# Norm arithmetic between the stages: from GpSimd to VectorE and ScalarE

## The chip, the cores and the metric

The kernel runs on one core of a Trainium2 chip. The core has five engines, each with its own instruction queue that it works off in order: TensorE (PE, matmuls and transposes; PEld is its weight load), VectorE (DVE), ScalarE (ACT), GpSimd (POOL) and SyncE (SP, which issues most of the DMAs). The metric is the device time of one execution in microseconds (us); of several runs the median is taken.

## What is computed

The reference is a transformer of three layers over 512 latent rows (and in its first layer 256 context rows) of 1024 columns. Each layer mixes the rows (windowed attention, a gated scan, then attention beside a state-space model) and sends them through an MLP or a mixture of experts. What matters here lies between these stages:

```python
def rms_norm(x, gain):
    xf = x.astype(jnp.float32)
    y = xf * lax.rsqrt(jnp.mean(xf * xf, axis=-1, keepdims=True) + NORM_EPS)
    return (y * gain.astype(jnp.float32)).astype(x.dtype)

def modulate(x, gain, shift, scale):
    return rms_norm(x, gain) * (1 + scale) + shift

def channel_mlp(h, w_in, w_out):
    return jnp.square(jax.nn.relu(h @ w_in)) @ w_out
```

After a stage with the result y, the rows become x = x + gate * rms_norm(y, gain), and the next stage reads h = modulate(x, ...). So there are two norms in a row at each change of stage: one over y (below: the postnorm) and one over the new x (the prenorm). All of it is in float32.

## The kernel before

**Precision.** A float32 matmul is made of three matmuls in a faster format. Each operand is split into a high half (a rounding cast, made by ScalarE) and a low half (the operand minus the high half, a subtraction of two tiles); then high x high, high x low and low x high are summed. For weights, `unit` does that for a block of 128 x 2048: the DMA brings `raw`, ScalarE casts `whi` (L233), VectorE subtracts `wlo` (L234). For the normed rows the high half is written at L321 and the low half at L322, into the tile pair `hl` (latent rows) or `hc` (context rows).

**Tiles.** Rows are worked on in tiles of 128: tiles 0 to 3 are latent, 4 and 5 are context. A stage's last matmuls go tile by tile. `finish` of a tile is issued one tile behind the matmuls that make it, so the norms of tile i stand beside the matmuls of tile i + 1, and those of the last tiles stand beside the first matmuls of the next stage.

**One tile's norms.** Postnorm: ScalarE squares y and sums the row (L331); `rsqrt` scales the sum on VectorE (L276) and takes the power -1/2 on GpSimd (L278, here called the root). Where y is in PSUM in two halves (after the out-projections) VectorE does L348 and L349 for each. Where y is one SBUF tile `acc` (after an MLP), one of two forms runs: with `pool`, GpSimd multiplies y by the gate (L342) and VectorE adds y times the root to x (L343); without it, VectorE does L339, which needs the root, and L340. Prenorm: ScalarE squares x (L291), VectorE L276, GpSimd the root, VectorE scales the row into `xn` (L300), TensorE transposes its eight 128 x 128 blocks (L308), and the columns of the result are scaled (and shifted) into the float32 scratch tile `h`: the first `dv` of the eight by VectorE (L312 or L314), the others by ScalarE (L317 or L319). Then the cast L321 and the subtraction L322, both of which read `h`.

**Buffers and order.** The scratch tiles junk, xn and h have one buffer each, so a tile's columns wait until L322 of the tile before has read h. The order of the instructions in each engine's queue is set when the kernel is built, by a scheduler that runs a timeline of all engines; a changed instruction can so move its neighbours. The first matmuls of layer 1 are those of `natproj` (L464 to L471): L468 is high x high, L469 high x low of the weights, L471 the low half of the rows. Accumulations of the MLP's result are L836.

Of the kernel before, what the change touches and what calls it, by code (L numbers as in the profile page):

```python
# [159 lines left out]
class Kern:  # L160
# [130 lines left out]
        self.nc.scalar.activation(junk[:, :n], x, AF.Square, accum_out=ss)  # L291
        return ss

    def prenorm(self, x, scale, shift, h, col, wide=True, dv=0, pool=False):

        nc = self.nc
        hi, lo = h
# [21 lines left out]
                nc.scalar.activation(f[:, k, :], b, AF.Identity, scale=scale[:, k:k + 1], bias=shift[:, k:k + 1])  # L319
        d = slice(col, col + P)  # L320
        self.norms.append((nc.scalar.copy(hi[:, :, d], f).ins, scaled))  # L321
        (nc.gpsimd if pool else nc.vector).tensor_sub(lo[:, :, d], f, hi[:, :, d].bitcast(F32))  # L322

    def postnorm(self, x, y, gate, pool=True):

        nc = self.nc
        ss2 = self.tiny(2)
        w = D // len(y)
        for n, b in enumerate(y):
            junk = self.s.tile([P, D], BF, tag="junk", name=self.nm("junk"))  # L330
            nc.scalar.activation(junk[:, :w], b, AF.Square, accum_out=ss2[:, n:n + 1])  # L331
        ss = ss2[:, 0:1]
        if len(y) == 2:
            ss = self.tiny(1)
            nc.vector.tensor_add(ss, ss2[:, 0:1], ss2[:, 1:2])  # L335
        r = self.rsqrt(ss, 1, D)
        if len(y) == 1:
            if not pool:
                nc.vector.scalar_tensor_tensor(y[0], y[0], r, gate, op0=ALU.mult, op1=ALU.mult)  # L339
                nc.vector.tensor_add(x, x, y[0])  # L340
                return
            nc.gpsimd.tensor_mul(y[0], y[0], gate)  # L342
            nc.vector.scalar_tensor_tensor(x, y[0], r, x, op0=ALU.mult, op1=ALU.add)  # L343
            return
        for n, b in enumerate(y):
            d = slice(n * w, n * w + w)
            t = self.s.tile([P, D], F32, tag="pn", name=self.nm("pn"))[:, d]
            nc.vector.scalar_tensor_tensor(t, b, r, gate[:, d], op0=ALU.mult, op1=ALU.mult)  # L348
            nc.vector.tensor_add(x[:, d], x[:, d], t)  # L349
# [508 lines left out]
def layer0(K):  # L858
# [5 lines left out]
    h = [None, None]  # L864
    hp, h_close = K.opened(K.left("h1l"))
    h[0] = K.pair(hp, "hl", [P, KC, L])
    pre = lambda i, sc, sh, wide=True, dv=0, pool=False: K.prenorm(X[i], sc[:, i // 4], sh[:, i // 4], h[i // 4], i % 4 * P, wide, dv, pool)
    with K.scratch(), K.right("gate") as gp:
        gates = []

        def finish(i, bs):
            if not gates:
                gates.extend(K.mod_gate(0, "mix", b, gp) for b in range(2))
            K.postnorm(X[i], bs, gates[i // 4])
            if i < 4:
                pre(i, sc, sh, dv=0, pool=i < 3)

        def loads():
            for i, x in enumerate(X):
                K.nc.sync.dma_start(x, A["x"][i] if i < 4 else A["ctx"][i - 4])  # L880
        out_full(K, A["w_o0"], [(i, ol, i) for i in range(4)] + [(4 + i, oc, i) for i in range(2)], finish,
                 pre=w_o, loaded=loads)
    K.opool.close()
    h[1] = K.pair(h_close.enter_context(K.left("h1c")), "hc", [P, KC, NCTX])
    with K.scratch(), K.right("gate") as gp:
# [11 lines left out]

        def finish2(i, y):
            K.postnorm(X[i], y, gates2[i // 4])
            pre(i, *K.aff[1, "mix"], dv=2, pool=i < 4)  # L900
        mw, mw_close = K.opened(K.left("mw"))
        mlp(K, 0, list(h), [4, 2], finish2, swap, "left", filler=K.mod_dots(gp, mw), steps=4)
    K.ctx_close.close()
# [274 lines left out]
def layer1(K, X, h, ssm):  # L1178
# [5 lines left out]
    with K.scratch(), K.right("gate") as gp:  # L1184
        gates = []

        def finish(i, bs):
            if not gates:
                gates.append(K.mod_gate(1, "mix", 0, gp))
            K.postnorm(X[i], bs, gates[0])  # L1190
            K.prenorm(X[i], sc[:, 0], sh[:, 0], h3, i * P, dv=3 if i > 1 else 0, pool=i < 1)
        out_full(K, K.A["w_o1"], [(i, oT, i) for i in range(4)], finish)
    K.opool.close()
    h = []
    with K.scratch(), K.right("gate") as gp:
# [8 lines left out]
            h.extend(K.pair(hp, "hl", [P, KC, L]))  # L1204

        def finish2(i, y):
            K.postnorm(X[i], y, gates2[0], i not in (0, 1, 3))
            K.prenorm(X[i], K.sm("mix_gain"), None, h, i * P, dv=2, pool=i < 3)
        tp, t_close = K.opened(K.left("ssmt"))
        mlp(K, 1, [h3], [4], finish2, swap, "left", True, ssm.constants(tp))  # L1210
    return h
# [939 lines left out]
```

## Time and profile before

| | us |
|---|---|
| median of 3 runs | 2224.25 |
| lowest, highest run | 2215.38, 2228.82 |
| the profiled execution: its time, its span | 2222.53, 2220.7 |
| TensorE busy | 2111.7 (95%) |
| VectorE busy | 1388.7 (63%) |
| ScalarE busy | 968.0 (44%) |
| GpSimd busy | 333.4 (15%) |
| mean granted TensorE clock | 0.980 |

The span runs from the first to the last instruction. In the rows, "0.39 PE L468 ..." is one instruction (or, with x2, several in a row) with its duration; "[1.61 <-DVE xn L300]" says that the engine was idle for 1.61 us before it, and what ended that. The granted clock is 1.00 at full speed (2.4 GHz) and 0.5 at the lower of its two levels (1.2 GHz); between these it is a mean over the window.

### The profile page before, as it was taken

The page shows a single profiled execution, that of the slowest core. Times are in us where ns is not written, and L with a number is a line of the kernel's source. Part 1 is how long each engine was busy: PE and PEld are TensorE (multiplying, and loading weights), DVE is VectorE, ACT ScalarE, POOL GpSimd, SP SyncE. Part 2 cuts the span into 40 slices and gives each one's busy share as a digit, 9 for nine tenths or more (in the row PEclk, how much of TensorE's full clock was granted, in tenths as well). Part 3 has the DMA queues.
Part 4 walks back from the last instruction along what each step waited for, and adds up shares of the span by engine and source line. Part 5 has one row for each costly group of instructions (what it writes and reads, how often), then busy time and mean ns, then how long its engine had stood idle before and what let it go on. Part 6 is the DMA issues. An engine that isn't in the chain of part 4 may idle for free. (4 is left out here: it accounts for less than half of the span.)

```text
span 2220.7 us, 28902 instructions
## 1 busy us (share of the span) xinstructions
PE 2111.7 (95%) x11224; PEld 1714.9 (77%) x11224; DVE 1388.7 (63%) x2420; ACT 968.0 (44%) x1484; POOL 333.4 (15%) x457
## 2 busy tenths in 40 slices
PE   6999999999999999999989999999999998988997
PEld 5976668888888888778877888888778875776765
DVE  4666765998654454541794588555637845747875
ACT  5446656421121121541654533232344546536775
POOL 0036632112000000420000100010130000012331
PEclk9999999999999999999999999999999998998999
DMA  7112241557421111111211224333322442678993
GB/s 297 58 39 81 111 152 40 198 189 249 140 68 61 62 65 61 63 57 57 98 39 39 83 83 148 117 106 127 122 102 100 141 157 74 227 260 277 315 304 96
DMA packets 54459, 281.11 MB, mean 127 GB/s; under 512 B 9200, under 2 KB 9600, under 8 KB 29360
## 3 DMA queue, kind: packets, MB, share of 16 engines
q1 hardware_dynamic: 33968, 219.39, 27.7%
q0 software_dynamic: 19344, 57.14, 8.3%
q10 hardware_dynamic: 1008, 2.70, 0.4%
q8 instruction: 90, 1.47, 0.3%
q14 instruction: 49, 0.40, 0.1%
HBM read 266.64 MB, written 26.18 MB: 132 GB/s over the span
## 5 line engine op out<-in xcount | busy, mean ns | idle before, releaser
L233 ACT CAST whi<-raw 128x2048 fp32r<-128x2048 f32 x106 | 202.6, 1912 | 587.8 <-PE b L264 382.8
L234 DVE TENSOR_TENSOR wlo<-raw,whi 128x2048 fp32r<-128x2048 f32 x106 | 245.2, 2314 | 221.0 <-ACT whi L233 220.5
L262 PE MATMUL b<-hl,whi 128*128 128x512 f32 (+1 forms) x736 | 283.9, 386 | 2.7 <-DVE t L335 1.6
L260 PE MATMUL b<-hl,whi 128*128 128x512 f32 (+1 forms) x736 | 283.5, 386 | 0.9 <-ACT whi L233 0.9
L264 PE MATMUL b<-hl,wlo 128*128 128x512 f32 (+1 forms) x736 | 281.1, 386 | 0.0
L836 DVE TENSOR_TENSOR acc<-acc,b 128x512 f32<-128x512 f32 x280 | 180.7, 682 | 146.9 <-PE b L264 146.8
L260 PE MATMUL b<-whi,hid 128*128 128x512 f32 x640 | 213.0, 391 | 3.1 <-ACT whi L233 1.9
L262 PE MATMUL b<-wlo,hid 128*128 128x512 f32 x640 | 214.3, 390 | 0.0
L264 PE MATMUL b<-whi,hid 128*128 128x512 f32 x640 | 211.7, 390 | 0.0
L262 PEld LDWEIGHTS b<-hl,whi 128*128 128x128 f32 x736 | 139.4, 189 | 30.8 <-issue 3.2
L264 PEld LDWEIGHTS b<-hl,wlo 128*128 128x128 f32 x736 | 139.4, 189 | 30.2 <-issue 2.0
L260 PEld LDWEIGHTS b<-hl,whi 128*128 128x128 f32 x736 | 139.2, 189 | 29.3 <-ACT whi L233 1.3
L2007 DVE TENSOR_TENSOR wlo<-raw,whi 128x2048 fp32r<-128x2048 f32 x57 | 129.9, 2287 | 32.9 <-ACT whi L2007 32.9
L260 PEld LDWEIGHTS b<-whi,hid 128*128 128x128 f32 x640 | 118.8, 188 | 27.5 <-ACT whi L233 2.1
L264 PEld LDWEIGHTS b<-whi,hid 128*128 128x128 f32 x640 | 120.0, 188 | 25.6
L262 PEld LDWEIGHTS b<-wlo,hid 128*128 128x128 f32 x640 | 120.1, 188 | 25.0
L2007 ACT CAST whi<-raw 128x2048 fp32r<-128x2048 f32 x57 | 108.3, 1912 | 10.2 <-PE b L254 10.1
L414 DVE CUSTOM_DVE_ANT_0 junk<-mw,cb 128x1024 bf16<-128x1024 f32 x80 | 97.5, 1219 | 6.9 <-DMA mw<-in_w_modT_dram 6.4
L645 POOL TENSOR_TENSOR p<-p,t 128x512 f32<-128x512 f32 (+2 forms) x96 | 94.0, 995 | 40.3 <-DVE t L644 37.6
L643 ACT ACTIVATE p<-p,t 128x513 f32<-128x513 f32 (+2 forms) x96 | 65.8, 687 | 50.7 <-DVE t L641 40.3
L641 DVE CUSTOM_DVE_ANT_0 p<-b,mask,nsink 128x512 f32<-128x512 f32 (+2 forms) x96 | 65.2, 701 | 27.9 <-PE b L637 23.6
L262 PE MATMUL b<-hc,whi 128*128 128x256 f32 x288 | 80.9, 281 | 0.0
(611 smaller groups left out, 4468.7 us busy)
## 6 DMA issues: line engine op xcount, KB each, us to landing
raw<-in_w_e_dram SPq DMA_DIRECT2D x57, 1024.0 KB, 7.2
raw<-in_w_mlp_in_dram SPq DMA_DIRECT2D x32, 1024.0 KB, 5.0
raw<-in_w_mlp_out_dram SPq DMA_DIRECT2D x32, 1024.0 KB, 4.9
mw<-in_w_modT_dram POOLq DMA_DIRECT2D x56, 512.0 KB, 4.5
raw<-in_w_mod_dram SPq DMA_DIRECT2D x20, 1024.0 KB, 6.6
raw<-in_w_in_dram SPq DMA_DIRECT2D x16, 1024.0 KB, 4.9
raw<-in_gla_in_dram SPq DMA_DIRECT2D x12, 1024.0 KB, 4.9
raw<-in_w_o_dram SPq DMA_DIRECT2D x8, 1024.0 KB, 4.9
```

Of the source, the lines that this page charges most:

```text
L233: ins = self.nc.scalar.copy(hi, r).ins
L234: ins = ins, (self.nc.gpsimd if pool else self.nc.vector).tensor_sub(lo, r, hi.bitcast(F32)).ins
L260: mm(o, ah, b, start=start, stop=False)
L262: mm(o, ah, b, start=False, stop=False)
L264: mm(o, al, b, start=False, stop=stop)
L414: v.tensor_tensor_reduce(junk, w, cb[b], 1.0, 0.0, ALU.mult, ALU.add, to[:, k, b:b + 1])
L641: nc.vector.tensor_tensor_reduce(p[:, :n], S[:, a0:a0 + n], added[:, z:z + n], -1.0, ns, ALU.add, ALU.min, nmx)
L643: nc.scalar.activation(p[:, :n + 1], p[:, :n + 1], AF.Exp, bias=nmx, scale=-1.0, accum_out=den)
L645: nc.gpsimd.tensor_mul(p[:, :n], p[:, :n], den.to_broadcast([P, n]))
L836: nc.vector.tensor_add(a, a, bs[n])
L2007: ins = K.nc.scalar.copy(hi, r).ins, K.nc.vector.tensor_sub(lo, r, hi.bitcast(F32)).ins
```

## The change

The argument `pool` goes from prenorm, postnorm and their callers, and `dv` = 2 from the two callers after the MLPs. The low halves of the normed rows (L322) are all subtracted on VectorE: 11 move from GpSimd, 3 after the out-projection of layer 0, 4 after its MLP, 1 after the out-projection of layer 1 and 3 after its MLP. The gate multiplication after an MLP is always its own instruction, on VectorE: 7 move from GpSimd (six tiles after the first MLP, tile 2 after the second), and for tiles 0, 1 and 3 after the second MLP the pair L339, L340 becomes a multiplication and one instruction that multiplies by the root and adds. After both MLPs (6 and 4 tiles) ScalarE does all eight columns. GpSimd keeps the roots. The line numbers of the changed file are 4 lower from L342 on: L342 becomes L338, L343 becomes L339, L836 becomes L832, L468 becomes L464.

```diff
--- before.py
+++ after.py
@@ -291,7 +291,7 @@
         self.nc.scalar.activation(junk[:, :n], x, AF.Square, accum_out=ss)
         return ss
 
-    def prenorm(self, x, scale, shift, h, col, wide=True, dv=0, pool=False):
+    def prenorm(self, x, scale, shift, h, col, wide=True, dv=0):
 
         nc = self.nc
         hi, lo = h
@@ -319,9 +319,9 @@
                 nc.scalar.activation(f[:, k, :], b, AF.Identity, scale=scale[:, k:k + 1], bias=shift[:, k:k + 1])
         d = slice(col, col + P)
         self.norms.append((nc.scalar.copy(hi[:, :, d], f).ins, scaled))
-        (nc.gpsimd if pool else nc.vector).tensor_sub(lo[:, :, d], f, hi[:, :, d].bitcast(F32))
-
-    def postnorm(self, x, y, gate, pool=True):
+        nc.vector.tensor_sub(lo[:, :, d], f, hi[:, :, d].bitcast(F32))
+
+    def postnorm(self, x, y, gate):
 
         nc = self.nc
         ss2 = self.tiny(2)
@@ -335,11 +335,7 @@
             nc.vector.tensor_add(ss, ss2[:, 0:1], ss2[:, 1:2])
         r = self.rsqrt(ss, 1, D)
         if len(y) == 1:
-            if not pool:
-                nc.vector.scalar_tensor_tensor(y[0], y[0], r, gate, op0=ALU.mult, op1=ALU.mult)
-                nc.vector.tensor_add(x, x, y[0])
-                return
-            nc.gpsimd.tensor_mul(y[0], y[0], gate)
+            nc.vector.tensor_mul(y[0], y[0], gate)
             nc.vector.scalar_tensor_tensor(x, y[0], r, x, op0=ALU.mult, op1=ALU.add)
             return
         for n, b in enumerate(y):
@@ -864,7 +860,7 @@
     h = [None, None]
     hp, h_close = K.opened(K.left("h1l"))
     h[0] = K.pair(hp, "hl", [P, KC, L])
-    pre = lambda i, sc, sh, wide=True, dv=0, pool=False: K.prenorm(X[i], sc[:, i // 4], sh[:, i // 4], h[i // 4], i % 4 * P, wide, dv, pool)
+    pre = lambda i, sc, sh, wide=True, dv=0: K.prenorm(X[i], sc[:, i // 4], sh[:, i // 4], h[i // 4], i % 4 * P, wide, dv)
     with K.scratch(), K.right("gate") as gp:
         gates = []
 
@@ -873,7 +869,7 @@
                 gates.extend(K.mod_gate(0, "mix", b, gp) for b in range(2))
             K.postnorm(X[i], bs, gates[i // 4])
             if i < 4:
-                pre(i, sc, sh, dv=0, pool=i < 3)
+                pre(i, sc, sh, dv=0)
 
         def loads():
             for i, x in enumerate(X):
@@ -897,7 +893,7 @@
 
         def finish2(i, y):
             K.postnorm(X[i], y, gates2[i // 4])
-            pre(i, *K.aff[1, "mix"], dv=2, pool=i < 4)
+            pre(i, *K.aff[1, "mix"])
         mw, mw_close = K.opened(K.left("mw"))
         mlp(K, 0, list(h), [4, 2], finish2, swap, "left", filler=K.mod_dots(gp, mw), steps=4)
     K.ctx_close.close()
@@ -1188,7 +1184,7 @@
             if not gates:
                 gates.append(K.mod_gate(1, "mix", 0, gp))
             K.postnorm(X[i], bs, gates[0])
-            K.prenorm(X[i], sc[:, 0], sh[:, 0], h3, i * P, dv=3 if i > 1 else 0, pool=i < 1)
+            K.prenorm(X[i], sc[:, 0], sh[:, 0], h3, i * P, dv=3 if i > 1 else 0)
         out_full(K, K.A["w_o1"], [(i, oT, i) for i in range(4)], finish)
     K.opool.close()
     h = []
@@ -1204,8 +1200,8 @@
             h.extend(K.pair(hp, "hl", [P, KC, L]))
 
         def finish2(i, y):
-            K.postnorm(X[i], y, gates2[0], i not in (0, 1, 3))
-            K.prenorm(X[i], K.sm("mix_gain"), None, h, i * P, dv=2, pool=i < 3)
+            K.postnorm(X[i], y, gates2[0])
+            K.prenorm(X[i], K.sm("mix_gain"), None, h, i * P)
         tp, t_close = K.opened(K.left("ssmt"))
         mlp(K, 1, [h3], [4], finish2, swap, "left", True, ssm.constants(tp))
     return h
```

The order of the queues changes with it. The first place is VectorE at the end of the first MLP, where tiles 1 to 3 are normed (x_3448 to x_3450 are the rows of tiles 1 to 3, acc the MLP's results, hl_8036 the low halves for layer 1, wlo_8474 its first weights). Before:

```order
L300 TENSOR_SCALAR xn_8181<-x_3448,t_8177 128x1024
L276 TENSOR_SCALAR t_8234<-t_8231 128x1
L343 SCALAR_TENSOR_TENSOR x_3449<-acc_4151,t_8235,x_3449 128x1024
L836 TENSOR_TENSOR acc_4153<-acc_4153,b_8271 128x512
L836 TENSOR_TENSOR acc_4153<-acc_4153,b_8272 128x512
L276 TENSOR_SCALAR t_8244<-t_8241 128x1
L276 TENSOR_SCALAR t_8302<-t_8299 128x1
L314 TENSOR_SCALAR h_8183<-b_1554_8184,aff_5846,aff_5847 128x128 x2
L300 TENSOR_SCALAR xn_8249<-x_3449,t_8245 128x1024
L343 SCALAR_TENSOR_TENSOR x_3450<-acc_4152,t_8303,x_3450 128x1024
```

and changed:

```order
L276 TENSOR_SCALAR t_8234<-t_8231 128x1
L338 TENSOR_TENSOR acc_4151<-acc_4151,gate_8003 128x1024
L832 TENSOR_TENSOR acc_4152<-acc_4152,b_8204 128x512
L339 SCALAR_TENSOR_TENSOR x_3449<-acc_4151,t_8235,x_3449 128x1024
L322 TENSOR_TENSOR hl_8036<-h_8115,hl_8035 128x8x128
L276 TENSOR_SCALAR t_8244<-t_8241 128x1
L300 TENSOR_SCALAR xn_8249<-x_3449,t_8245 128x1024
L832 TENSOR_TENSOR acc_4153<-acc_4153,b_8271 128x512
L832 TENSOR_TENSOR acc_4153<-acc_4153,b_8272 128x512
L276 TENSOR_SCALAR t_8302<-t_8299 128x1
L338 TENSOR_TENSOR acc_4152<-acc_4152,gate_8003 128x1024
L339 SCALAR_TENSOR_TENSOR x_3450<-acc_4152,t_8303,x_3450 128x1024
```

The multiplication L338 and the subtraction L322 stand in VectorE's queue now, the two columns L314 are gone, and the xn of tile 2 (xn_8249) stands ahead of the accumulation into acc_4153 instead of behind it.

The second place is TensorE there: the last matmuls of the MLP (b_8339, b_8340), the transposes of tile 2 (xn_8249), and the first matmuls of layer 1. Before:

```order
L262 MATMUL b_8339<-wlo_7997,hid_1503_7976 128x512
L262 MATMUL b_8340<-wlo_7997,hid_1503_7976 128x512
L264 MATMUL b_8339<-whi_7996,hid_1504_7977 128x512
L264 MATMUL b_8340<-whi_7996,hid_1504_7977 128x512
L308 MATMUL b_1569_8252<-ident,xn_8249 128x128 x8
L468 MATMUL b_8483<-whi_8473,hl_8035 128x512
```

and changed:

```order
L262 MATMUL b_8339<-wlo_7997,hid_1503_7976 128x512
L262 MATMUL b_8340<-wlo_7997,hid_1503_7976 128x512
L308 MATMUL b_1569_8252<-ident,xn_8249 128x128 x8
L264 MATMUL b_8339<-whi_7996,hid_1504_7977 128x512
L264 MATMUL b_8340<-whi_7996,hid_1504_7977 128x512
L464 MATMUL b_8483<-whi_8473,hl_8035 128x512
```

The transposes stand two matmuls earlier; the rest has the same order.

The third place is VectorE at the end of the second MLP, tiles 1 and 2 (x_3448, x_3449). Before:

```order
L836 TENSOR_TENSOR acc_10643<-acc_10643,b_13351 128x512
L836 TENSOR_TENSOR acc_10643<-acc_10643,b_13352 128x512
L312 TENSOR_SCALAR h_13263<-b_2390_13264,small 128x128 x2
L276 TENSOR_SCALAR t_13324<-t_13321 128x1
L276 TENSOR_SCALAR t_13382<-t_13379 128x1
L300 TENSOR_SCALAR xn_13329<-x_3448,t_13325 128x1024
L343 SCALAR_TENSOR_TENSOR x_3449<-acc_10642,t_13383,x_3449 128x1024
L312 TENSOR_SCALAR h_13331<-b_2405_13332,small 128x128 x2
L276 TENSOR_SCALAR t_13392<-t_13389 128x1
```

and changed:

```order
L832 TENSOR_TENSOR acc_10643<-acc_10643,b_13351 128x512
L832 TENSOR_TENSOR acc_10643<-acc_10643,b_13352 128x512
L276 TENSOR_SCALAR t_13324<-t_13321 128x1
L276 TENSOR_SCALAR t_13382<-t_13379 128x1
L338 TENSOR_TENSOR acc_10642<-acc_10642,gate_13151 128x1024
L300 TENSOR_SCALAR xn_13329<-x_3448,t_13325 128x1024
L339 SCALAR_TENSOR_TENSOR x_3449<-acc_10642,t_13383,x_3449 128x1024
L322 TENSOR_TENSOR hl_13186<-h_13263,hl_13185 128x8x128
L276 TENSOR_SCALAR t_13392<-t_13389 128x1
L300 TENSOR_SCALAR xn_13397<-x_3449,t_13393 128x1024
```

The xn of tile 1 (xn_13329) stands behind the multiplication for tile 2 now, and the subtraction for tile 0 (h_13263) ahead of the xn of tile 2.

## Rows read from the trace of the kernel before

**Rows 1.** Windows around seam B: length, busy us (count) of PE, PEld, DVE, ACT, POOL, granted clock.

```profile
890.00:930.80 40.80, 40.80 (x209) 34.48 (x208) 21.95 (x32) 17.03 (x30) 14.34 (x11) 1.00 0.07 26
930.80:945.00 14.20, 9.01 (x28) 6.26 (x27) 11.55 (x10) 13.32 (x22) 10.62 (x7) 0.76 0.41 140
945.00:968.00 23.00, 21.11 (x104) 17.29 (x105) 16.35 (x17) 14.61 (x27) 12.16 (x9) 1.00 0.14 46
```

**Rows 2.** TensorE's timeline, seam B: start, duration, line, out<-in, idle before, its releaser.

```profile
932.60 1.06 PE L308 MATMUL b<-ident,xn 128*128 128x128 f32 x8 [1.61 <-DVE xn L300]
...
937.63 0.80 PE L469 MATMUL b<-wlo,hl 128*128 128x512 f32 x1 [1.73 <-DVE t L276]
938.23 0.63 PE L468 MATMUL b<-whi,hl 128*128 128x512 f32 x1
...
945.24 0.39 PE L468 MATMUL b<-whi,hl 128*128 128x512 f32 x1
...
967.65 0.50 PE L468 MATMUL b<-whi,hc 128*128 128x512 f32 x1 [1.63 <-ACT hc L321]
```

**Rows 3.** TensorE's timeline, seams A and D.

```profile
388.47 0.47 PE L262 MATMUL b<-hl,whi 128*128 128x512 f32 x1 [1.59 <-DVE t L335]
...
1612.59 1.94 PE L308 MATMUL b<-ident,xn 128*128 128x128 f32 x8 [5.46 <-DVE xn L300]
...
1636.63 0.80 PE L468 MATMUL b<-ya,hl 128*128 128x512 f32 x1 [2.52 <-ACT hl L321]
```

**Rows 4.** VectorE's timeline, seam B.

```profile
912.58 0.75 DVE L300 TENSOR_SCALAR xn<-x,t 128x1024 f32<-128x1024 f32 x1 [0.73 <-POOL t L278]
...
920.63 2.25 DVE L300 TENSOR_SCALAR xn<-x,t 128x1024 f32<-128x1024 f32 x1
...
923.67 3.41 DVE L343 SCALAR_TENSOR_TENSOR x<-acc,t,x 128x1024 f32<-128x1024 f32 x1 [0.73 <-POOL t L278]
...
929.56 0.73 DVE L314 TENSOR_SCALAR h<-b,aff,aff 128x128 f32<-128x128 f32 x2
930.21 2.25 DVE L300 TENSOR_SCALAR xn<-x,t 128x1024 f32<-128x1024 f32 x1
932.89 1.29 DVE L343 SCALAR_TENSOR_TENSOR x<-acc,t,x 128x1024 f32<-128x1024 f32 x1 [0.44 <-POOL less L935]
...
935.29 2.29 DVE L234 TENSOR_TENSOR wlo<-raw,whi 128x2048 fp32r<-128x2048 f32 x1
...
940.50 4.35 DVE L234 TENSOR_TENSOR wlo<-raw,whi 128x2048 fp32r<-128x2048 f32 x1
```

**Rows 5.** GpSimd's timeline, seam B.

```profile
919.92 2.40 POOL L342 TENSOR_TENSOR acc<-acc,gate 128x1024 f32<-128x1024 f32 x1 [0.38 <-ACT junk L331]
...
940.33 2.38 POOL L342 TENSOR_TENSOR acc<-acc,gate 128x1024 f32<-128x1024 f32 x1
```

**Rows 6.** Line L322: engine, operation, count: shortest/median/longest ns, first and last start.

```profile
L322 POOL TENSOR_TENSOR hl<-h,hl x11: 2349/2677/4387, 348.8 to 1628.3; 128x1024 fp32r<-128x1024 f32 x11
...
L322 DVE TENSOR_TENSOR hl<-h,hl x5: 1215/1219/1226, 387.1 to 1636.6; 128x1024 fp32r<-128x1024 f32 x5
```

**Rows 7.** ScalarE's timeline, seams B and C.

```profile
927.11 1.06 ACT L291 ACTIVATE junk<-x 128x1024 bf16<-128x1024 f32 x1 [4.08 <-DVE x L343]
...
930.41 2.21 ACT L319 ACTIVATE h<-b,aff,aff 128x128 f32<-128x128 f32 x6 [0.96 <-DVE h L314]
...
1219.17 2.91 ACT L319 ACTIVATE h<-b,aff,aff 128x128 f32<-128x128 f32 x8 [3.23 <-PE b L308]
```

**Rows 8.** GpSimd's roots and one VectorE row, from their timelines, seams A and B.

```profile
394.37 1.52 POOL L278 TENSOR_TENSOR t<-t,mhalf 128x1 f32<-128x1 f32 x1 [4.54 <-DVE t L276]
...
394.26 1.22 DVE L414 CUSTOM_DVE_ANT_0 junk<-mw,cb 128x1024 bf16<-128x1024 f32 x1
...
908.54 0.56 POOL L278 TENSOR_TENSOR t<-t,mhalf 128x1 f32<-128x1 f32 x1
```

**Rows 9.** VectorE's timeline, seam D.

```profile
1609.57 2.87 DVE L300 TENSOR_SCALAR xn<-x,t 128x1024 f32<-128x1024 f32 x1
```

## The prediction

> **What bounds the kernel now.** I read the windows first, then TensorE's timeline in the seams, then the three engines that feed it. In the windows [rows 1] the reader sees a kernel that is TensorE's: between 890 and 930.8 us it is busy 40.80 of 40.80 us. Vector, Scalar and GpSimd work costs nothing while that holds. It stops holding where one stage ends in a norm and the next needs the normed rows. I call the four such places seam A (out-projection of layer 0 to its MLP, 372 to 410), B (end of that MLP to layer 1, 930.8 to 968), C (out-projection of layer 1 to its MLP, 1205 to 1244) and D (end of that MLP to block 2, from 1606). The change touches nothing but the norms at these seams, so all that it can give or take lies there.
>
> The idle time of a window is its length less TensorE's busy time. In B it is 14.20 - 9.01 = 5.19 and 23.00 - 21.11 = 1.89, together 7.08 [rows 1]. In A one wait of 1.59 stands for it, in D one of 5.46 and a later one of 2.52 [rows 3]. Idle time also costs clock: in 930.8 to 945 the granted clock is 0.76 on average [rows 1]. The same 512-column matmul takes 0.63 us at 938.23 and 0.39 at 945.24 [rows 2]. About 14 of them run so, and in a queue that starts one every 0.43 instead of every 0.23 us that is some 3 us more. At D the eight transposes take 1.94 us after the wait of 5.46, against 1.06 in B [rows 2, 3].
>
> TensorE's own timeline says what it waits for: the normed rows xn of VectorE's L300 (932.60, 1612.59), the weights' low halves (937.63; the row names the root's input L276, but the matmul reads wlo of L234), the high half of the normed rows from ScalarE (967.65, 1636.63) [rows 2, 3]. Then I ask why these are late. VectorE's rows show the same instruction at two lengths: xn takes 0.75 us alone (912.58) and 2.25 at 920.63 and 930.21. The L343 instruction takes 1.29 alone (932.89) and 3.41 at 923.67, and the wlo subtraction at 940.50 takes 4.35 [rows 4]. Each long one lies beside a two-input GpSimd instruction over 1024 columns: the gate multiplication at 919.92 or 940.33, 2.4 us each [rows 5]. The xn that starts at 920.63 ends at 922.88, 0.55 us after the multiplication's end at 922.32: most of it is waiting. So at the seams GpSimd doesn't relieve VectorE; it holds it.
>
> **The change, part by part.** (1) Eleven subtractions L322 move from GpSimd, 2.35 to 4.39 us each, to VectorE, where the same line takes 1.22 [rows 6]. The scratch tile h which they read has one buffer, so the next tile's ScalarE columns come free 1.1 to 3.2 us sooner. (2) Seven gate multiplications move likewise: 2.40 us there [rows 5], and I take 1.22 on VectorE, since the nearest row has the same inputs and shape [rows 6]. (3) At three tiles of D two VectorE instructions become two others of the same size, the first of which no longer needs the root: nothing, or up to 0.8 us of waiting saved. (4) Ten tiles at B and D lose their two VectorE columns, 0.73 us a pair (929.56) [rows 4], and ScalarE does eight in 2.91 instead of six in 2.21, so 0.70 more a tile [rows 7].
>
> VectorE's own account is 18 x 1.22 = 22.0 more, 10 x 0.73 = 7.3 less: 14.7 us. Against it stands the waiting in its long instructions. In B alone, by the rows shown, that is 1.50 for each of two xn, 2.12 for L343 and 2.06 for the wlo (4.35 against the 2.29 at 935.29, where VectorE came first and GpSimd second): 8.7; in D 2.87 - 0.75 = 2.1 for one xn [rows 9]. Counting the rows of that kind which are not shown I estimate 13 in B and 4.7 in D. The account is even; what changes is when the results come.
>
> *Seam B.* Before, the squares of tile 2 were in at about 919.5 (GpSimd's wait at 919.92 ends 0.38 after them [rows 5]), but its L276 stood behind the long xn until 922.8, and L343 ended at 927.08. ScalarE idled 4.08 us up to 927.11 for exactly that [rows 7]. Changed, xn takes 0.75; then come L276, the multiplication (1.22), an accumulation (0.64) and L339 (1.28), done near 923.5. Squares, root and xn (1.3 + 0.15 + 0.7 + 0.75) bring the xn of tile 2 to about 926.4 instead of 932.46. TensorE is free for it at 932.60 - 1.61 = 931.0, so that wait goes. ScalarE's whole row of casts starts some 3.5 us sooner, so the first weight's high half comes at about 931; 2.29 on VectorE bring its low half to 933 (before 935.29 + 2.29 = 937.6). For the next low half I get 938 (before 940.50 + 4.35 = 944.85). I keep three waits of 0.8 to 1 us, 2.5 together, because ScalarE is busy 13.32 of 14.20 us in this window [rows 1]. From 7.1 idle and 3 of low clock that leaves a gain of **7.5** (5 to 9).
>
> *Seam D.* The xn that ended at 1612.44 starts behind the multiplication now, but takes 0.75: it ends near 1610.6, 1.9 us sooner. The 2.52 at 1636.63 waits for the last tile's high half, which stood behind two slow GpSimd subtractions; with 1.22 each it is ready at about 1629, before TensorE asks. With it go the eight slow matmuls behind it, 1.6. Sum 6.0, less half a microsecond for roots that come later (below): **5.5** (3 to 7).
>
> *Seam A.* Three subtractions come to VectorE; the transposes of the fourth tile stand four matmuls earlier in TensorE's queue, so 4 x 0.23 of the 1.59 wait [rows 3] is covered: **0.8** (0 to 1). *Seam C.* One subtraction more on VectorE, 1.22 [rows 6], between steps that TensorE reads soon after; I take less than half of it: **-0.5** (0 to -1.2). *Elsewhere* some instructions change places with no edit behind it; 0, with one wait such as that at 1636.63 coming or going (+-2.5).
>
> *The roots.* They stay on GpSimd, and VectorE's two-input work now surrounds them. A root takes 0.56 us (908.54), but 1.52 at 394.37, where it starts 0.11 behind a VectorE instruction of 1.22 [rows 8]. At four tiles of B and D the multiplication directly precedes the instruction that needs the root, and I count 0.5 us on VectorE for each. Little reaches TensorE.
>
> Sum: 7.5 + 5.5 + 0.8 - 0.5 = 13.3. The profiled execution took 2222.5 us, so 2209; the runs' median of 2224.25 is 1.7 above it, so against that I would read 2211. I say **2210**.
>
> **The rivals.** *ScalarE is late next* (0.18). It is the fullest engine in 930.8 to 945 and gets 10 x 0.70 = 7.0 us more, while GpSimd's going helps it only through the buffer. If all of that lies on the path, the gain is 6.3: 2216. For it: its share of 94%. Against it: 4.08 us of idle time just before [rows 7], and 0.96 per tile in which it waited for VectorE's two columns.
>
> *The roots are held everywhere* (0.10). If each of the twenty roots of B and D loses the 0.96 between 1.52 and 0.56, and the ten of them at the tiles where TensorE waits show in full, 9.6 us go and the gain is 3.7: 2219. The Trainium skill, page "SBUF — State Buffer", section "SBUF: two separate sides", says that VectorE and GpSimd share one pair of ports as an exclusive lock, that a VectorE instruction with two SBUF inputs takes it against a GpSimd instruction that reads SBUF, and that whoever comes second is blocked for the whole instruction. By that rule the trace agrees, with 0.56 turned to 1.52; it would make each such root wait for the rest of a multiplication.
>
> *VectorE becomes the bound, slower* (0.09). If its instructions stay as long as they are for another reason than GpSimd (DMA traffic, say), its account at the seams is 14.7 us longer, and xn and wlo come later tile by tile: 2222.5 + 14.7 = 2237. It decides if the wlo at 940.50 ends later than 944.85. For it: VectorE is busy 11.55 of 14.20 us there [rows 1]. Against it: the short rows of the same lines [rows 4]. The Trainium skill, page "Perfetto Trace Analysis", section "Optimizing Scalar/DVE Operations", says that with VectorE saturated it may make sense to move work to ScalarE or even GpSimd, which this change reverses; it adds that the shared port may leave nothing of that, and the rows above show the second case.
>
> **How the numbers follow.** The forecast has 0.63; its own bounds are 5 + 3 + 0 - 1.2 - 2.5 = 4 and 9 + 7 + 1 + 2.5 = 19.5, thus 2203 to 2218 from the profiled time. The first two rivals reach 2219. The shown runs lie from 2215 to 2229 by themselves, so I widen by a few microseconds: **2199 to 2226**, which leaves the third rival out. One per cent, about what a measurement of this kernel can tell from no change, is 22 us: 2202 and 2246. Faster than that takes every upper bound at once (0.10); slower takes the third rival and more (0.03); 0.87 between.
>
> **What would show it.** Right: no xn or wlo over 1 and 2.5 us at B and D; GpSimd without instructions of 1024 columns there; TensorE's idle time between 930 and 968 at 2 to 3 us instead of 7.1, with the clock at 1.00; the wait near 1612 at about 3.5, that near 1636 gone. Wrong: a new wait in B on ScalarE's casts over 2 us, roots of 1.2 us or more in front of each xn, or an xn that is still 2 us with GpSimd silent.

## The result

The changed kernel takes 2200.64 us, the median of four runs (2196.43 to 2203.02), the kernel before 2224.18: a ratio of 0.9895, with a 95% interval of 0.9877 to 0.9913. That is 23.5 us less (19 to 27) where 14 were forecast. The profiled execution took 2196.43 us, the shortest of the four. The engines on its page (its span is 2194.6 us):

```profile
PE 2099.2 (96%) x11224; PEld 1710.7 (78%) x11224; DVE 1386.0 (63%) x2418; ACT 973.5 (44%) x1504; POOL 294.4 (13%) x439
```

The windows that hold the work of [rows 1], with the same columns. The seam's work starts 0.3 us earlier than before and ends 9 us earlier, so the windows are shorter:

```profile
889.50:930.20 40.70, 40.70 (x210) 34.51 (x209) 24.04 (x35) 22.28 (x40) 7.23 (x7) 1.00 0.07 26
930.20:937.10 6.90, 5.96 (x30) 4.46 (x29) 6.90 (x7) 6.90 (x13) 2.91 (x3) 1.00 0.65 243
937.10:959.00 21.90, 20.69 (x103) 17.26 (x104) 14.20 (x17) 18.56 (x35) 5.08 (x7) 1.00 0.17 62
```

The work that took 14.20 us takes 6.90, that of 23.00 takes 21.90. TensorE's idle time at seam B is 0.94 in the second window instead of 5.19, and 1.21 instead of 1.89 in the third. The clock is 1.00 throughout instead of 0.76 in the second, and GpSimd's 14.34, 10.62 and 12.16 us have become 7.23, 2.91 and 5.08. TensorE's waits, to be read against [rows 2, 3] (at 388 seam A, up to 952 B, at 1600 D):

```profile
388.13 0.50 PE L262 MATMUL b<-hl,whi 128*128 128x512 f32 x1 [0.56 <-DVE hl L322]
...
932.34 0.50 PE L465 MATMUL b<-wlo,hl 128*128 128x512 f32 x1 [0.27 <-DVE wlo L234]
...
936.93 0.50 PE L465 MATMUL b<-wlo,hl 128*128 128x512 f32 x1 [0.67 <-DVE wlo L234]
...
952.46 1.06 PE L308 MATMUL b<-ident,xn 128*128 128x128 f32 x8 [1.21 <-DVE xn L300]
...
1600.52 1.97 PE L308 MATMUL b<-ident,xn 128*128 128x128 f32 x8 [3.34 <-DVE xn L300]
```

In A 1.59 became 0.56. In B three waits are left, 2.15 together: two on low halves of weights and one on an xn. In D the wait of 5.46 is 3.34, with the eight transposes behind it as slow as before (1.97), and that of 2.52 is gone. VectorE at B, against [rows 4]:

```profile
919.53 1.22 DVE L338 TENSOR_TENSOR acc<-acc,gate 128x1024 f32<-128x1024 f32 x1
...
924.70 0.76 DVE L300 TENSOR_SCALAR xn<-x,t 128x1024 f32<-128x1024 f32 x1 [0.79 <-POOL t L278]
...
930.00 2.29 DVE L234 TENSOR_TENSOR wlo<-raw,whi 128x2048 fp32r<-128x2048 f32 x1 [0.42 <-ACT whi L233]
...
934.60 2.28 DVE L234 TENSOR_TENSOR wlo<-raw,whi 128x2048 fp32r<-128x2048 f32 x1
```

No xn takes more than 0.95, and the wlo take 2.29 and 2.28. At D the xn of tile 1 takes 0.75 behind the multiplication for tile 2, against 2.87 in [rows 9]:

```profile
1598.59 1.22 DVE L338 TENSOR_TENSOR acc<-acc,gate 128x1024 f32<-128x1024 f32 x1
1599.72 0.75 DVE L300 TENSOR_SCALAR xn<-x,t 128x1024 f32<-128x1024 f32 x1
```

GpSimd has only roots there. They are longer than the 0.56 of [rows 8]:

```profile
919.77 1.39 POOL L278 TENSOR_TENSOR t<-t,mhalf 128x1 f32<-128x1 f32 x1 [1.59 <-DVE t L276]
...
934.77 2.52 POOL L278 TENSOR_TENSOR t<-t,mhalf 128x1 f32<-128x1 f32 x1 [2.43 <-DVE t L276]
```

The first starts 0.24 behind the multiplication that VectorE begins at 919.53, the second 0.17 behind the wlo subtraction of 934.60, and both end 0.41 after it. ScalarE, against [rows 7]:

```profile
922.58 1.06 ACT L291 ACTIVATE junk<-x 128x1024 bf16<-128x1024 f32 x1 [0.23 <-DVE x L339]
...
924.82 2.89 ACT L319 ACTIVATE h<-b,aff,aff 128x128 f32<-128x128 f32 x8
```

The wait of 4.08 for the new x is 0.23, and the eight columns take 2.89.

**Where the time went.** Both programs give TensorE the same number of matmuls, 11224 in either trace. Take the start of the k-th in one trace less that of the k-th in the other: what this difference gains over a stretch is what the stretch gained. The table has it for every profile, against the first profile of the kernel before. Negative is shorter, in us; the stretches outside the seams are named by the times of the kernel before. The last column is the median of the runs less that of the kernel before beside it.

| kernel | A | B | C | D | 1820 to 1930 | from 2060 | median |
|---|---|---|---|---|---|---|---|
| changed | -1.0 | -8.75 | 0.0 | -5.9 | -4.1 | -6.6 | -23.5 |
| changed, again | -1.0 | -8.7 | 0.0 | -7.0 | -1.3 | -5.8 | one run |
| before, again | 0.0 | 0.0 | 0.0 | -0.1 | 0.1 | 1.6 | one run |
| e1 first MLP | 0.0 | -8.9 | 0.0 | -0.1 | -2.6 | 0.2 | -10.7 |
| e2 second MLP | 0.0 | 1.5 | 0.0 | -5.8 | -2.8 | -8.1 | -10.1 |
| e3 subtractions | -1.0 | -6.2 | 0.0 | -4.0 | 0.0 | 5.4 | -9.6 |
| e4 multiplications | 0.0 | -3.8 | 0.0 | -5.9 | -3.2 | -5.2 | -14.2 |
| e5 without columns | -1.0 | -5.2 | 0.0 | -6.8 | 1.1 | -9.3 | -14.8 |
| e6 xn first | -1.0 | -8.75 | 0.0 | -8.2 | 1.4 | -9.2 | -21.9 |
| e9 two old splits | -1.0 | -8.75 | 0.0 | -5.9 | -4.1 | 0.9 | -22.2 |
| e10 two splits | 0.0 | 0.0 | 0.0 | -0.1 | 0.4 | 0.7 | 1.7 |
| e11 three splits | 0.0 | 1.5 | 0.0 | 0.0 | -1.9 | 0.7 | -2.5 |
| e12 multiplications back | -1.0 | -2.4 | 0.0 | -6.9 | -1.3 | 2.7 | -10.0 |

The four seams give 15.7 us (16.7 in the second profile of the changed kernel), and the forecast was 13.3. The other 7 or so lie, by these profiles, in two places that the forecast set to nothing. Sums of a row can differ from the median by some microseconds, since a row is one execution.

### The profile page after: what moved, and what is told of

Its sections match the earlier page's. It is cut to its first block, busy times and chain, and to the rows that moved or that the text cites. A ratio compares the mean times of both kernels' runs of the same rounds, so it can differ in the third digit from the quotient of the medians.

```text
span 2194.6 us, 28892 instructions
## 1 busy us (share of the span) xinstructions
PE 2099.2 (96%) x11224; PEld 1710.7 (78%) x11224; DVE 1386.0 (63%) x2418; ACT 973.5 (44%) x1504; POOL 294.4 (13%) x439
## 5 line engine op out<-in xcount | busy, mean ns | idle before, releaser
L832 DVE TENSOR_TENSOR acc<-acc,b 128x512 f32<-128x512 f32 x280 | 180.5, 682 | 146.3 <-PE b L264 146.1
L278 POOL TENSOR_TENSOR t<-t,mhalf 128x1 f32<-128x1 f32 (+1 forms) x54 | 43.3, 804 | 564.8 <-DVE t L276 564.7
```

What stands on the lines that cost most here:

```text
L278: self.nc.gpsimd.tensor_tensor(y, x, self.mhalf[:, :n], op=ALU.pow)
L832: nc.vector.tensor_add(a, a, bs[n])
```

## The experiments

**Each seam alone.** Two kernels keep the edits of one seam and leave the others as before; the first is

```diff
-            K.postnorm(X[i], y, gates2[i // 4])
-            pre(i, *K.aff[1, "mix"], dv=2, pool=i < 4)
+            K.postnorm(X[i], y, gates2[i // 4], None)   # None: multiplication on VectorE
+            pre(i, *K.aff[1, "mix"], dv=0)
```

and the second the same with D's two calls.

> Only the norms after the first MLP (seam B) are changed: their gate multiplications and low-half subtractions on VectorE, all eight columns on ScalarE; seams A, C, D as before. The changed kernel's TensorE gained 8.75 us at B, 5.9 at D, 1.0 at A, 4 in block 2 (its attention and state-space part) and 6 in the last 100 us. If the seams act alone: B gives 8 to 9 us, A, C and D nothing, and the time is 9 below the kernel before. Rival: the gains outside the seams (block 2 and the end) belong to the change as a whole; then they fail to appear here, or appear in part. Rival: they are scatter between executions; then this profile shows some other amount there, in either direction, of up to 6 us.

> Only the norms after the second MLP (seam D) are changed in that way; A, B, C as before. If the seams act alone: D gives 5 to 6.5 us, B nothing, and the time is 6 below the kernel before. If the 4 us in block 2, which follows D, come from D's change (through the order of the queues behind it), it is 10 below, and the first kernel of this call lacks them.

Measured: 2212.83 against 2223.51 us (ratio 0.9955, 0.9938 to 0.9971), and 2213.44 (0.9952, 0.9937 to 0.9968). B alone gives 8.9 and leaves D as it was; D alone gives 5.8 and leaves B, to the 1.5 us by which it also moves without an edit (below, under Scatter). TensorE's waits at B in the first:

```profile
932.87 0.50 PE L469 MATMUL b<-wlo,hl 128*128 128x512 f32 x1 [0.26 <-DVE wlo L234]
...
937.46 0.50 PE L469 MATMUL b<-wlo,hl 128*128 128x512 f32 x1 [0.65 <-DVE wlo L234]
...
952.78 1.07 PE L308 MATMUL b<-ident,xn 128*128 128x128 f32 x8 [1.01 <-ACT hl L321]
```

They are as long as those of the changed kernel, to 0.2 us, though the third row names another releaser. So the seams act by themselves. But the stretch from 2060 on is 0.2 longer in the first and 8.1 shorter in the second: that part does not go with B. Between 1820 and 1930 both gain alike, 2.6 and 2.8.

**Subtractions alone, multiplications alone.** VectorE keeps two columns in both.

```diff
-            pre(i, *K.aff[1, "mix"], dv=2, pool=i < 4)
+            pre(i, *K.aff[1, "mix"], dv=2)
```

(the same at the other three seams) and, in the second, only

```diff
-            nc.gpsimd.tensor_mul(y[0], y[0], gate)
+            (nc.gpsimd if pool else nc.vector).tensor_mul(y[0], y[0], gate)   # pool=None at B and D
```

> Only the eleven subtractions of the low halves move to VectorE; gate multiplications stay on GpSimd, and VectorE keeps two columns. Theory (VectorE is held by whatever GpSimd computes over 1024 columns): xn and the postnorm's last instruction stay at 2 us and more where a multiplication lies beside them, B gives 2 to 4 of its 8.75 us. Rival (what counted was the scratch tile h, held by GpSimd's slow subtraction): B gives 6 or more, D 4 or more.

> Only the gate multiplications after both MLPs move to VectorE (at D also the new pair of instructions for all tiles); the subtractions stay on GpSimd, and VectorE keeps two columns. Theory: xn takes 0.75 us again unless a subtraction lies beside it, B gives 4 to 6 us, D 2 to 4, more than the subtractions alone. Rival (scratch tile h): B and D give under 2.5 each, since h is held as long as before.

Measured: 2213.88 us (0.9950, 0.9934 to 0.9966) and 2209.34 (0.9936, 0.9923 to 0.9950). VectorE's groups at B in the kernel before (count, busy us, mean ns of one, idle time before):

```profile
L343 DVE SCALAR_TENSOR_TENSOR x<-acc,t,x 128x1024 f32<-128x1024 f32 x6 | 12.0, 1993 | 4.2 <-POOL t L278 3.8 <-POOL less L935 0.4
L300 DVE TENSOR_SCALAR xn<-x,t 128x1024 f32<-128x1024 f32 x6 | 9.6, 1593 | 1.4 <-POOL t L278 1.4
...
L234 DVE TENSOR_TENSOR wlo<-raw,whi 128x2048 fp32r<-128x2048 f32 x2 | 6.6, 3317 | 0.0
```

with the subtractions moved:

```profile
L300 DVE TENSOR_SCALAR xn<-x,t 128x1024 f32<-128x1024 f32 x6 | 9.6, 1601 | 3.1 <-POOL t L278 3.1
L343 DVE SCALAR_TENSOR_TENSOR x<-acc,t,x 128x1024 f32<-128x1024 f32 x6 | 7.7, 1285 | 3.8 <-POOL t L278 3.7
...
L234 DVE TENSOR_TENSOR wlo<-raw,whi 128x2048 fp32r<-128x2048 f32 x2 | 4.6, 2284 | 0.0
```

and with the multiplications moved:

```profile
L343 DVE SCALAR_TENSOR_TENSOR x<-acc,t,x 128x1024 f32<-128x1024 f32 x6 | 9.8, 1634 | 0.9 <-POOL t L278 0.9
...
L300 DVE TENSOR_SCALAR xn<-x,t 128x1024 f32<-128x1024 f32 x6 | 5.0, 840 | 2.1 <-POOL t L278 2.1
L234 DVE TENSOR_TENSOR wlo<-raw,whi 128x2048 fp32r<-128x2048 f32 x2 | 4.6, 2282 | 0.0
```

The xn is long (1.60 on average) as long as the multiplication is on GpSimd, and nearly whole (0.84) without it; the instruction L343 is long where the subtraction is (1.63), and whole (1.29) without it. Each of VectorE's instructions is held by whatever GpSimd instruction lies beside it: that part of the theory stands. Its ranking does not: at B the subtractions give 6.2 and the multiplications 3.8. The first is what the rival on the scratch tile h asked for (6 or more, and 4 or more at D); the second is more than it allowed (under 2.5), and less than the theory's 4 to 6. What h cost stands in a row of VectorE in the kernel before, at B:

```profile
939.85 0.73 DVE L314 TENSOR_SCALAR h<-b,aff,aff 128x128 f32<-128x128 f32 x2 [2.21 <-POOL hl L322]
```

VectorE waits 2.21 us until GpSimd's subtraction of 4.39 lets go of h, and the wlo of 940.50 stands behind that. The one edit ends this wait and makes L343 whole; how the 6.2 divides between the two is not shown, since no kernel with a second buffer for h was run. At D it is the other way, 4.0 and 5.9, and TensorE's rows say which edit ends which wait. Subtractions moved, then multiplications moved:

```profile
1608.55 1.94 PE L308 MATMUL b<-ident,xn 128*128 128x128 f32 x8 [5.46 <-DVE xn L300]
...
1624.52 0.50 PE L468 MATMUL b<-ya,hl 128*128 128x512 f32 x1 [0.75 <-ACT hl L321]
```

```profile
1606.80 1.94 PE L308 MATMUL b<-ident,xn 128*128 128x128 f32 x8 [3.43 <-DVE xn L300]
```

The wait of 5.46 stays until the multiplication goes (3.43); the wait of 2.52 falls to 0.75 with the subtractions, and is gone with the multiplications alone too.

**The columns.** The changed kernel with `dv=2` at B and D again:

```diff
-            pre(i, *K.aff[1, "mix"])
+            pre(i, *K.aff[1, "mix"], dv=2)
```

> The changed kernel, but VectorE keeps two of the eight columns at B and D as before the change. My theory gives the columns no share of the gain: ScalarE does eight in 2.9 us instead of six in 2.2 at B, VectorE loses 0.73 a tile, so B and D change by under 1 us in either direction. Rival (ScalarE's wait for VectorE's columns was a cause): B loses 2 us or more of its 8.75.

Measured: 2208.67 us (0.9935, 0.9912 to 0.9959). B gives 5.2 instead of 8.75, so the rival was right and I was wrong: the columns are worth 3.5 us at B, and nothing at D. ScalarE and TensorE at B:

```profile
939.05 2.21 ACT L319 ACTIVATE h<-b,aff,aff 128x128 f32<-128x128 f32 x6 [2.55 <-DVE t L276]
...
946.70 2.21 ACT L319 ACTIVATE h<-b,aff,aff 128x128 f32<-128x128 f32 x6 [2.06 <-DVE h L314]
```

```profile
954.37 1.66 PE L308 MATMUL b<-ident,xn 128*128 128x128 f32 x8 [2.81 <-DVE xn L300]
```

ScalarE waits 2.55 and 2.06 us for VectorE's two columns of a tile (the first row names the instruction next to them); they stand in VectorE's queue behind the weight subtraction and the multiplication. Behind them ScalarE squares the next tile's new rows (L291) at 948.77, where it does so at 947.03 in the changed kernel. The root and the xn follow later, and TensorE's wait for that xn is 2.81 instead of 1.21.

**The multiplications at B, taken back.** The last question on B was whether VectorE, which now is fuller, would do better without them:

```diff
-            nc.vector.tensor_mul(y[0], y[0], gate)
+            (nc.gpsimd if pool else nc.vector).tensor_mul(y[0], y[0], gate)   # pool=True at B
```

> The changed kernel, but at B the six gate multiplications are back on GpSimd; the subtractions stay on VectorE, the eight columns on ScalarE, D as changed. With the subtractions alone B gave 6.2 us, with subtractions and multiplications but two columns on VectorE 5.2, with all three 8.75. Theory A (VectorE's queue is the short one at B once GpSimd no longer holds h; taking 7.3 us of multiplications from it is worth more than the holding of xn costs): B gives 8.75 to 9.5, as much as the change or more, with xn at 1.6 us on average and no wait on a weight's low half over 0.7. Theory B (any GpSimd work over 1024 columns costs VectorE what it lasts): B gives 6 to 7.5, the time is 2 us above the changed kernel's.

Measured: 2211.60 against 2221.63 us (0.9957, 0.9943 to 0.9971). B gives 2.4, less than both theories allowed. TensorE, GpSimd and VectorE:

```profile
936.78 0.50 PE L465 MATMUL b<-wlo,hl 128*128 128x512 f32 x1 [2.49 <-DVE wlo L234]
...
958.32 1.29 PE L308 MATMUL b<-ident,xn 128*128 128x128 f32 x8 [3.60 <-DVE xn L300]
```

```profile
939.39 2.93 POOL L338 TENSOR_TENSOR acc<-acc,gate 128x1024 f32<-128x1024 f32 x1 [6.01 <-ACT junk L331]
942.28 2.09 POOL L278 TENSOR_TENSOR t<-t,mhalf 128x1 f32<-128x1 f32 x2
...
948.13 2.41 POOL L338 TENSOR_TENSOR acc<-acc,gate 128x1024 f32<-128x1024 f32 x1 [0.38 <-ACT junk L331]
```

```profile
937.78 2.28 DVE L234 TENSOR_TENSOR wlo<-raw,whi 128x2048 fp32r<-128x2048 f32 x1
939.99 0.14 DVE L276 TENSOR_SCALAR t<-t 128x1 f32<-128x1 f32 x1
940.05 3.09 DVE L943 TENSOR_TENSOR wd<-wd,wd 128x768 fp32r<-128x768 f32 x1
...
948.17 2.92 DVE L300 TENSOR_SCALAR xn<-x,t 128x1024 f32<-128x1024 f32 x1
```

Besides holding the xn (2.92), the multiplication holds the roots that stand behind it in GpSimd's own queue: the one that VectorE's row at 939.99 asks for starts at 942.28. And the holding goes both ways in turn: at 939.39 the multiplication takes 2.93 itself, since VectorE's weight subtraction of 937.78 lasts until 940.06; then it holds VectorE's next subtraction, which takes 3.09 here and 0.95 in the changed kernel. So the parts don't add up. Subtractions alone give 6.2, with multiplications 5.2 (no difference, to the 1.5 us of scatter), with columns 2.4, and with both 8.75.

**xn first.** One swap on VectorE at D:

```diff
-            nc.vector.tensor_mul(y[0], y[0], gate)
+            m = nc.vector.tensor_mul(y[0], y[0], gate).ins   # and m is put behind the xn of the tile before
```

> The changed kernel with one swap at D: the xn of tile 1 stands ahead of the gate multiplication for tile 2 on VectorE instead of behind it. xn then starts when its root is there, 1.1 us sooner, and TensorE's wait there goes from 3.34 to about 2.2 us; the eight transposes still run at the lower clock. D gives 7 instead of 5.9, the time is 1 us lower, inside what the comparison can tell. Rival: the root for tile 2, held by the multiplication that now comes later, makes the next xn later and takes it back in another wait.

Measured: 2201.52 us (0.9903, 0.9886 to 0.9920), no difference from the changed kernel that the runs can tell. TensorE at D:

```profile
1598.99 1.09 PE L308 MATMUL b<-ident,xn 128*128 128x128 f32 x8 [2.25 <-DVE xn L300]
1601.24 0.50 PE L467 MATMUL b<-ya,hl 128*128 128x512 f32 x1 [1.15 <-ACT hl L321]
```

The wait fell from 3.34 to 2.25, as expected, and one of 1.15 came in behind it, on ScalarE's high half. Idle time is the same, but split in two it didn't cost clock: the eight transposes take 1.09, not the lower clock's time that I had expected. The windows around it, with the swap and in the changed kernel:

```profile
1585.00:1600.00 15.00, 12.75 (x64) 10.42 (x62) 11.86 (x19) 7.71 (x18) 6.03 (x7) 1.00 0.33 108
1600.00:1612.00 12.00, 10.85 (x52) 8.89 (x52) 7.92 (x11) 11.27 (x28) 3.41 (x4) 1.00 0.16 63
```

```profile
1587.00:1602.00 15.00, 11.66 (x57) 9.77 (x56) 11.83 (x18) 7.85 (x18) 6.77 (x7) 0.91 0.31 115
1602.00:1614.00 12.00, 12.00 (x51) 9.78 (x50) 6.39 (x10) 10.28 (x26) 3.51 (x4) 0.83 0.06 24
```

The granted clock stays at 1.00, where it was 0.91 and 0.83, and that makes the table's 8.2 for D against 5.9 and 7.0.

**Scatter.** Both kernels once more under the profiler, without an edit:

> The kernel before, unchanged, once more under the profiler. The seams of the changed kernel account for 15.7 us of 26.5 between the two profiles; 4.1 lie in block 2's part between 1820 and 1930 and 6.6 after 2060. Scatter theory: this profile differs from the first of the same kernel by up to 5 us in just these two stretches and by under 0.3 in the four seams. Rival (those gains belong to the change): it agrees with the first within 1 us there too.

> The changed kernel, unchanged, once more under the profiler. Scatter theory: the seams again give 0.9, 8.8, 0 and 5.9 us, and the stretches 1820 to 1930 and from 2060 on move by some microseconds against its first profile, towards the kernel before, since that first profile was of its fastest run. Rival: within 1 us of the first profile everywhere.

Measured: 2226.20 and 2197.48 us, one run each. A, B and C repeat to 0.05 us in both, D to 1.1; but B is 1.5 longer in e2 and e11, where it is unchanged, so a single seam of a single profile is good to that. From 1820 to 1930 the changed kernel moves by 2.8 and from 2060 on by 0.8; the kernel before by 0.1 and 1.6. The scatter is real, but in these four profiles it doesn't bridge the gap from 2060 on (0 and 1.6 against -6.6 and -5.8).

**The order of the last stage.** There the planner (the scheduler that sets the queues' order) has put three weight splits (the 48th, 52nd and 55th of 57) ahead of one neighbour each, on ScalarE, and two of them on VectorE. Nothing was edited there; it picks this order in the changed kernel, e2, e4, e5 and e6, and the old one in e1, e3 and e12. Three kernels set it by hand:

```diff
+    PAIRS = [(("split", 52), ("rows", 19)), (("split", 55), ("down", 17))]   # e9, e10; e11 also (("split", 48), ("hidden", 16))
+                for a, b in zip(seen[second], seen[first]):
+                    self.K.tc.add_manual_dep(a, b.name, ...)
```

> The changed kernel, with two weight splits of the last stage (the 52nd and the 55th of 57) put back behind the operations that they stood behind before the change; nothing else moves on any engine. Theory (the change's gain after 2060 comes in part from this order, which the builder's planner picks anew when the norms after the second MLP get shorter): the wait of 1.8 us that both profiles of the kernel before show some 21 us before their end (TensorE on the low half of a weight) comes back, and the stretch from 2060 on loses 2 to 4 of its 6 us. Rival (scatter of the weight transfers alone): no such wait, and that stretch stays within 3 us of the changed kernel's two profiles.

> The kernel before, with only those two weight splits put ahead of the operations that they stood behind; nothing else moves on any engine. Order theory: the wait of 1.8 us near the end goes, the stretch from 2060 on is 2 to 4 us shorter, A to D are unchanged, the time is 2 to 4 us below the kernel before. Scatter theory: the wait stays or the stretch moves by under 1.6 us, as between the two profiles of the kernel before.

> The kernel before, with all three weight splits that the change moved (the 48th too) put ahead; here the planner also moves ten of TensorE's instructions in that stage forward by a few places. Order theory: 2 to 6 us shorter from 2060 on, at least as much as with two. Scatter theory: as there.

Measured: 2201.17 us (0.9899, 0.9860 to 0.9939), 2225.01 (0.9998, 0.9978 to 1.0018) and 2220.84 (0.9982, 0.9965 to 0.9999). TensorE near the end, in the kernel before (its second profile) and in the changed kernel with two old splits:

```profile
2203.33 0.50 PE L253 MATMUL b<-wlo,x 128*128 128x512 f32 x1 [1.82 <-DVE wlo L2007]
```

```profile
2177.86 0.50 PE L253 MATMUL b<-wlo,x 128*128 128x512 f32 x1 [1.83 <-DVE wlo L2016]
```

The wait of 1.8 goes with the order: it came back in the changed kernel and went from the kernel before. Matched matmul by matmul, the work that starts between 2195.5 and 2206 in the kernel before is 2.1 us shorter in all eight profiles in which the 52nd and the 55th split stand ahead, e10 and e11 among them, and in none of the others. But the stretch as a whole didn't follow in the kernel before: between 2148 and 2172 e10 lost 3.9 and e11 2.7. In e10 a wait 34 us ahead had grown to 3.40, where 1.59 and 1.55 stand in the two profiles of the kernel before:

```profile
2171.27 0.49 PE L252 MATMUL b<-whi,x 128*128 128x512 f32 x1 [3.40 <-ACT whi L2020]
```

In the changed kernel it did follow: with two old splits the stretch lost 7.5 us, all of its gain of 6.6 and more, where the order theory asked for 2 to 4. The times decide nothing: e9's median is near the changed kernel's, but uncertain by 9 us; e10 shows no gain, within 4 us; e11 shows one of 4 us (0.2 to 7.8) by its ratio, which is what the theory asked for, though its profile is of the slowest of its ten executions. So the swaps end one wait and are worth 2 us where it stood. That they carry the whole of the stretch's gain is neither shown nor ruled out.

## Why the prediction was right, and where not

*The bound and the mechanism* were right in the main: the gain in the seams comes with GpSimd's instructions no longer holding VectorE's, and with h coming free sooner, which part (1) of the change had; the shares are not shown. One reading was off: the L343 of 923.67 lies not beside a multiplication but beside the subtraction that GpSimd starts at 923.60 (2.40 long). And one sum was off: the waiting in VectorE's long rows shown for B is 7.2 us, not 8.7. Nothing hangs on it: by the groups of the two runs above, with the subtractions or the multiplications moved, L343 gets 4.3 us shorter, xn 4.6 and wlo 2.0, 10.9 where I had estimated 13 with the rows not shown, and VectorE's busy time stayed even (1386.0 after 1388.7). The rule of the Trainium skill's page "SBUF — State Buffer", section "SBUF: two separate sides", that the second comer is blocked, is what the two roots (1.39 and 2.52) and the xn of 2.92 show.

*Seam B*, forecast 7.5, measured 8.75. The xn of tile 2 was due at 926.4 and came at 925.46 (the changed kernel runs 0.3 us ahead there); the low halves at 933 and 938 came at 932.29 and 936.88. The waits left, 2.5 by the forecast, are 2.15. The size was right for a reason that was partly wrong: I gave the columns no share, by setting 0.73 us off VectorE against 0.70 on ScalarE. Undone, they cost 3.5. The row with ScalarE's 0.96 us of waiting for them [rows 7] was in my hands; I used it only against a rival.

*Seam D*, forecast 5.5, measured 5.9 and 7.0. The xn was due 1.9 us sooner; the wait became 2.1 shorter, and the second one went with its slow matmuls. *Seam A* gave 1.0 for 0.8, *seam C* nothing for a loss of 0.5.

*The roots* are held much as the second rival had it: at B the postnorm's roots take 1.4 us and more instead of 0.56. That rival still failed, because the instruction that needs the root stands behind the multiplication anyway: most of the root's waiting lies beside it, and VectorE then idles 0.44 us for it at three tiles of six.

*ScalarE late next* failed, though ScalarE and VectorE are busy for all 6.90 us of the seam's second window: no wait of TensorE at B in the changed kernel goes to ScalarE's casts directly, and only the one of 0.27 indirectly, through a wlo that waited 0.42 for its cast. *VectorE the bound, slower* failed: VectorE's long rows at B are short once GpSimd has only the roots (xn 0.95 at most, wlo 2.29), and no part of the change that was run makes B slower (5.2 gained with two columns on VectorE, 2.4 with the multiplications on GpSimd).

*Elsewhere, nothing (+-2.5)*: this is the step that failed, by about 7 us in the medians and 10.7 in the first pair of profiles. The two stretches before and after (length, busy times, granted clock, as in [rows 1]):

```profile
1820.00:1930.00 110.00, 101.25 (x584) 72.86 (x583) 65.07 (x136) 67.09 (x108) 2.29 (x13) 0.92 0.42 148
2060.00:2220.70 160.70, 138.38 (x636) 108.24 (x635) 117.02 (x83) 108.91 (x97) 43.25 (x25) 0.97 0.73 236
```

```profile
1804.00:1914.00 110.00, 98.86 (x601) 71.69 (x599) 68.52 (x140) 66.30 (x108) 2.32 (x13) 0.98 0.44 157
2040.00:2194.60 154.60, 136.85 (x638) 109.99 (x636) 117.41 (x84) 109.73 (x98) 44.32 (x26) 0.95 0.75 246
```

In the first stretch TensorE is idle for longer than before (11.1 against 8.75 us), but the granted clock is 0.98 against 0.92, and the window holds 17 more matmuls. The planner changed the order of the attention work there. Over the same matmuls the idle time goes with that order: 8.7 to 9.4 us in the seven profiles with the old one, 10.9 to 11.7 in the seven with the new. The clock doesn't: 0.92 to 0.95 with the old order, 0.91 to 0.98 with the new, and 0.98 and 0.95 in the two profiles of the changed kernel itself. So the stretch lies between 2.6 gained and 0.4 lost with the old order, between 4.1 gained and 1.4 lost with the new, and its gain is not shown to be the change's. From 2060 on nearly the same work (two matmuls more) is 6.1 us shorter (154.6 against 160.7). Every kernel for which the planner itself chose the new order of splits has 5 to 9 us there, every one with the old order none (0.2 to 5.4 longer); setting two or three of them by hand gave 2.1 us at one place and nothing over the stretch. What carries the rest I have not found, and it stays open. In the medians, what is left after the seams is a gain of 7 to 8 us for the changed kernel and of 2 to 6 for e2, e4, e5 and e6; for e1, e3 and e12 it is between 1.7 gained and 1.6 lost. Each of these is uncertain by 3 to 5. For e9, with two old splits, it is 6.5, uncertain by 9.

I had seen that the order changes there and priced it at nothing, because no edit stood behind it. The gain as a whole came out at 1.05%, just beyond the 1% to which I had given a chance of 0.10. That the time lies in the range at all is luck: 2200.64 is under the 2203 that the terms' own bounds gave, and inside only by what I had added for the spread of the runs.

## What to carry to other kernels

Where two engines can each do a small elementwise step, look for the same instruction at two lengths: if VectorE's grow whenever GpSimd computes, moving the work to VectorE can cost it nothing. Price a shared tile by who waits for whom in both queues, not by the durations that change sides; parts of such a change can gain far less than the whole (2.4 of 8.75 at B), so test the whole before the parts. With a planner that sets every queue's order, read what it moved in stages without an edit too, and profile each kernel twice before giving such a stage's gain to the change.

## What the hardware showed

A GpSimd instruction on one column per partition, 0.56 us alone, lasts 1.39 us behind a VectorE multiplication of 1.22 and 2.52 behind a VectorE subtraction of 2.28, and ends 0.41 after it each time. The holding goes both ways in turn: a GpSimd multiplication of 2.40 took 2.93 behind a VectorE subtraction that had begun earlier, and then held VectorE's next one, 0.95 long, for 3.09. And one program ran the same matmuls of the third attention part at mean granted clocks of 0.98 and 0.95 in two executions, with the same 11.1 us of idle time.
